# A two-layer decoder trunk on one core: the planner gets other lengths, and the side steps are spread between the parts of a pair

## The chip, the cores and the metric

The kernel runs on one core of one Trainium2 chip. The time is device microseconds (us) of one execution of the whole program; several runs are given by their median. TensorE is called PE, VectorE DVE, ScalarE ACT, GpSimd POOL and SyncE SP; SP issues nearly all DMAs. Smaller is better.

## The reference

The input is one sequence of 1024 tokens with 1024 features in float32. Two layers follow each other; each has a token mixer and a SwiGLU, and each of these four sub-layers reads a normed x that is scaled and shifted by vectors computed from a conditioning vector c (`mod`), and is added back with a gate from the same.

```python
for i in range(DEPTH):                      # 2
    mod = silu(c) @ ada_w[i] + ada_b[i]     # six vectors of 1024
    sh1, sc1, g1, sh2, sc2, g2 = split(mod, 6)
    h = rmsnorm(x, norm1_g[i]) * (1 + sc1) + sh1
    y = dsa_mixer(h) if i == 0 else short_conv_mixer(h)
    x = x + g1 * y
    h = rmsnorm(x, norm2_g[i]) * (1 + sc2) + sh2
    x = x + g2 * ((silu(h @ w_gate[i]) * (h @ w_up[i])) @ w_down[i])   # 2816 hidden
```

The first mixer is a sparse attention: eight index heads score every key for every query (`relu(qi . ki)`, weighted and summed), the 256 best keys of a query are kept, and 16 heads with 4 key heads attend to those only. The second mixer is a gated causal convolution of width 3: `(b * conv(c * u)) @ w_out`.

## The kernel before

**Planner.** The code doesn't call the engines. It records operations into a `Plan`, with the operations that each depends on, and a list scheduler (`drain`) then issues them: it keeps a modelled clock for PE, DVE, ACT, POOL and SP, takes at each step the engine that can start first, and on it the ready operation with the lowest priority number. The priority is the place in the program, or a number that the code sets (`plan.pri`). So the order of instructions on each engine follows from the lengths that `cost` and `record` give to operations, from the delays between engines (`LATENCY`, `SLACK`), from the landing time of a DMA (1.6 us beyond its transfer at 380 KB per us), and from `CHANGE`, a charge on PE when the form of the stationary operand changes. `copy` operations may go to ACT or DVE, as the modelled clock has it. On the chip, each engine runs its instructions in the order in which they were issued, and waits at each until its operands are there.

**Products.** Most products are float32 split into a rounded high part and a rest: `whi` (a cast, mostly ACT) and `wlo` (a subtraction, DVE), and three matmuls for each (`mm3`), 512 columns wide.

**Stages.** First x is read and turned, the first conditioning vectors are made, and h is formed. Then come the projections: the index keys, the index queries (`rope_pair`, stored to DRAM by `to_dram` as `qid` and loaded back by `index` as `q` in the tile `karena`), keys, queries and values. `index` computes the row products of index queries and keys (`pair_products`, two matmuls with 64 rows each side by side into the bank `ps_L`), ACT applies the relu, and DVE sums into `sc`. `select` finds the 256th best score by 31 rounds of counting, on DVE or ACT. Attention (`attend`) goes by blocks of 128 queries: row products into `ps_L`, mask and maximum on DVE (tiles `p`, `mx`), exponential on ACT, transposes on PE, copies `pf`, products with the values into `ps_o`. The out projection is laid between the later blocks.

**Tail.** The SwiGLUs and the convolution use products by halves with seven instead of eight block products (class `Pair`: `first`, `second`, `rest`, `third`, `fourth`; pairs that had two products made early finish in `done`). In the SwiGLU one gate pair and one up pair make a step of 256 hidden columns, eleven steps in all. `row_sums` and `hidden` store results (`t`, `hid`) to DRAM for the down product. Beside this run *side steps*: `side_step` loads a block `adaw` of the conditioning weights (SP, three buffers) and adds its product with c to an accumulator `cv` (DVE); after eight of them PE turns the accumulator (`ada_turned`, four transposes with `ident`, a reduction on DVE). The first SwiGLU makes six of the vectors (96 loads), the second one (16). From the ninth pair on, eight side steps (four in the second SwiGLU) are recorded after a pair's use.

Of the kernel before, what the change touches and what calls it, by code (L numbers as in the profile page):

```python
# [161 lines left out]
class Plan:  # L162
# [4 lines left out]
    WINDOW = 3.41  # L167
    BIAS = 0.8
    CHANGE = 0.15
    STAY = 4.0  # L170

    def __init__(self, nc, tc):
        self.nc, self.tc, self.pri, self.count = nc, tc, None, 0
        for e in self.ENGINES:
            setattr(self, e, Engine(self, e))
        self.free = dict.fromkeys(self.ENGINES, 0.0)
        self.soon = {e: [] for e in self.ENGINES}
        self.now = {e: [] for e in self.ENGINES}
        self.dma = self.window = self.busy = 0.0
        self.slow = 2.0  # L180
        self.gate = self.form = None
# [25 lines left out]
    def cost(self, eng, fn, out, ins, kw):  # L207

        n = out.free
        if fn == "dma_start":  # L210
            if eng == "gpsimd":
                return 0.85, 1.6
            inside = len(ins) == 1 and all(r.store.alloc is not None for r in ins + [out])
            return {"sync": 0.65 if inside else 0.475, "scalar": 0.1}[eng], 1.6
        if eng == "tensor":
            if fn == "transpose":
                return 0.107, 0.0
            if ins[1].dtype in (F32R, BF16):
                return max(n, 64) * 17 / 38400.0, 0.0
            return max(n * 4, 512) / (4800.0 if HD in (ins[0].free, ins[0].shape[0]) else  # L220
                                      2400.0), 0.0
# [3 lines left out]
        if eng == "scalar":  # L225
            return 0.03 + 0.95e-3 * n + (0.09 if "accum_out" in kw else 0.0) + 0.1 * aps, 0.0
# [30 lines left out]
    def matmuls(self, calls, rate, start=True, stop=True):  # L257
# [9 lines left out]
        op = Op("tensor", rate * calls[0][0].free, emit, (self.pri, self.count))  # L267
# [5 lines left out]
    def record(self, eng, fn, args, kw, other=None):  # L273
# [17 lines left out]
        if fn == "dma_start":  # L291
            op.lat = lat + shaped.free * shaped.shape[0] * 4 / 380e3
# [99 lines left out]
    def drain(self, *pools):  # L392

        held = []
        while any(p.pending for p in pools) if pools else True:
# [44 lines left out]
            if op.lat:  # L440
                self.dma = max(self.dma, end) + (op.lat - 1.6)
                end = self.dma + 1.6
                if e == "sync":
                    self.free[e] = max(self.free[e], self.dma - 2.5)
# [11 lines left out]
HW = 512  # L456
# [354 lines left out]
class Attention:  # L811
# [225 lines left out]
    def to_dram(self, t, dram, j, two, half, sl):  # L1037
        rows = dram.part_of((half, j, two))[2 * P * j:2 * P * (j + 1), sl]
        self.nc.sync.dma_start(rows.rearrange("(h a q) t -> a h q t", a=2, q=32)[two], t)
# [90 lines left out]
    def pair_products(self, q, k, wd, use):  # L1130

        for c0 in range(0, wd, HW):
# [4 lines left out]
            self.plan.matmuls([(ps[r], q[rows[r]], k[rows[r], cs]) for r in range(2)], 2.057e-3)  # L1137
# [227 lines left out]
class Tail:  # L1365
# [4 lines left out]
    EARLY, KEPT, SIDE = 10, 4, (8, 4)  # L1370
# [4 lines left out]
    def __init__(self, tk, ada_w, xspill):  # L1375
        self.tk, self.nc, self.plan, self.ada_w = tk, tk.nc, tk.plan, ada_w
        plan = tk.plan
        plan.pri = None
# [137 lines left out]
    def side_steps(self, layer):  # L1516
        for _ in range(self.SIDE[layer]):
            self.side_step()
# [175 lines left out]
    def pairs(self, pairs, use):  # L1694

        last = None
        for n, p in enumerate(pairs):
            if p.began:
                use(n, p.done())
                continue  # L1700
            p.first()
            if last is not None:
                last.fourth()
            p.second()
            if last is not None:
                use(n - 1, last.third())
            p.rest()
            last = p
# [3 lines left out]
    def ffn(self, layer, w_gate, w_up):  # L1712
# [4 lines left out]
        def use(n, rows):  # L1717
# [17 lines left out]
            if n >= 8:  # L1735
                self.side_steps(layer)
# [11 lines left out]
    def conv(self, w_in):  # L1748
# [14 lines left out]
        def conved(n, cs, us):  # L1763
            for f in range(2):
                i = 2 * n + f
                cw = [tk.vec[:, R_CW + j * 8 + i:R_CW + j * 8 + i + 1] for j in range(3)]
                for half in range(NH):
# [8 lines left out]
                    nc.vector.tensor_scalar(y, z[:, 0:HW], cw[0], None, op0=ALU.mult)  # L1776
# [20 lines left out]
    def run(self, w_gate, w_up, w_down, w_in, w_out, out):  # L1797
        self.side = self.side_list([(0, 5), *((1, j) for j in range(5))])
        self.ffn(0, w_gate[0], w_up[0])
# [3 lines left out]
        self.side = self.side_list([(1, 5)])  # L1803
        self.ffn(1, w_gate[1], w_up[1])
# [157 lines left out]
```

## Time and profile before

| | |
|---|---|
| median of 3 runs | 2303.0 us (2300.35 to 2303.5) |
| the profiled execution | 2300.25 us, span 2298.5 us |
| busy share of the span: PE, DVE, ACT | 97%, 79%, 49% |
| mean granted clock of PE | 0.991 |
| moved by DMA | 356.39 MB, mean 155 GB/s |

A row of a stretch of time gives its length and, for each engine, how long it was busy and with how many instructions, then the clock that PE was granted (1.00 is full speed), the busy share of the 16 DMA engines, and GB/s. A row of the timeline gives the start, the length, the engine, the operation with its output and inputs, and in brackets how long the engine stood idle before and what ended that. A row of waits gives who waited for whom, the sum, how many times, and the longest. A row of a group gives the busy time and mean length of its instructions, and the idle time just before them. Matmuls overlap in PE, so their lengths (0.39 us) are longer than the distance of their starts.

### The profile page before, as it was taken

How to read it: one execution, taken by the hardware profiler on the slowest of the kernel's cores; microseconds unless marked ns; L12 is line 12 of the kernel's file. 1: busy time of each engine (PE TensorE's matmuls, PEld its weight loads, DVE VectorE, ACT ScalarE, POOL GpSimd, SP SyncE). 2: the span in 40 equal slices, each digit the busy share in tenths (PEclk: the TensorE clock that was granted, in tenths of full speed). 3: DMA queues.
4: the chain of work that ended last, by engine and by line, in shares of the span. 5: the costliest groups of instructions: out<-in, count | busy, mean ns of one | idle time of the engine just before them, and what ended most of it. 6: DMA issues, size and time to landing. Idle time of an engine off the chain costs nothing.

```text
span 2298.5 us, 33032 instructions
## 1 busy us (share of the span) xinstructions
PE 2239.1 (97%) x11686; PEld 1812.2 (79%) x11686; DVE 1822.3 (79%) x3716; ACT 1116.4 (49%) x2137; POOL 5.6 (0%) x19
## 2 busy tenths in 40 slices
PE   7999999999999999999999999999999999999998
PEld 6667876876798887778888887778888878888887
DVE  6879999776478898888678899886798976667774
ACT  4576899756755333333344552234453233343444
POOL 0000000000000000000000000000000000000000
PEclk8999999999999999999999999999999999999999
DMA  8423343332244566655984154325345633349733
GB/s 299 128 65 94 91 120 98 105 92 66 74 126 136 175 209 201 221 185 187 362 298 168 55 147 129 115 89 173 110 140 181 197 107 110 111 152 388 275 125 97
DMA packets 334192, 356.39 MB, mean 155 GB/s; under 512 B 18089, under 2 KB 218826, under 8 KB 334026
## 3 DMA queue, kind: packets, MB, share of 16 engines
q1 hardware_dynamic: 332586, 352.96, 47.6%
q8 instruction: 92, 1.51, 0.3%
q10 hardware_dynamic: 1440, 1.31, 0.2%
q14 instruction: 74, 0.61, 0.1%
HBM read 282.64 MB, written 71.57 MB: 154 GB/s over the span
## 4 chain that ended last, share of the span: by engine, by line
PE 62%; DVE 18%; DMA 9%; issue 8%; ACT 2%; SPq 0%; POOL 0%; DVEq 0%; ACTq 0%; POOLq 0%
PE ps_x L244 24%; PE ps_mm L244 17%; PE ps_z L244 12%; PE ps_sm L244 5%; DVE s L244 3%; DVE u L244 3%; DVE wlo L244 3%; DMA raw<-in_ffn_w_gate_dram 2%; PE ps_L L244 2%; PE ps_o L244 2%; DVE v L244 2%; DMA adaw<-in_ada_w_dram 2%; DMA raw<-in_conv_w_in_dram 2%; DMA raw<-in_ffn_w_up_dram 2%; DVE cv L244 2%
## 5 line engine op out<-in xcount | busy, mean ns | idle before, releaser
L244 ACT CAST whi<-s 128x512 fp32r<-128x512 f32 x312 | 193.1, 621 | 452.5 <-issue 128.0
L244 PE MATMUL ps_x<-t,whi 128*128 128x512 f32 x1016 | 315.2, 391 | 8.6 <-ACT v L244 7.3
L244 ACT CAST whi<-raw 128x512 fp32r<-128x512 f32 (+1 forms) x245 | 149.6, 617 | 273.6 <-PE ps_z L244 68.7
L244 DVE TENSOR_TENSOR wlo<-s,whi 128x512 fp32r<-128x512 f32 x312 | 212.8, 685 | 46.5 <-ACT whi L244 45.9
L244 PEld LDWEIGHTS ps_x<-t,whi 128*128 128x128 f32 x1016 | 189.2, 188 | 50.6 <-ACT v L244 9.4
L244 DVE TENSOR_TENSOR wlo<-raw,whi 128x512 fp32r<-128x512 f32 (+1 forms) x254 | 172.7, 683 | 66.1 <-ACT whi L244 65.3
L244 PE MATMUL ps_x<-t,wlo 128*128 128x512 f32 x508 | 198.2, 390 | 0.2 <-DVE wlo L244 0.2
L244 PE MATMUL ps_x<-h,whi 128*128 128x512 f32 x536 | 165.6, 390 | 0.0
L244 PE MATMUL ps_z<-t,whi 128*128 128x512 f32 x488 | 150.3, 389 | 0.0
L244 DVE CUSTOM_DVE_ANT_0 p<-ps_L,bias 128x512 f32<-128x512 f32 (+3 forms) x192 | 99.7, 551 | 38.4 <-PE ps_L L244 23.7
L244 PE MATMUL ps_z<-h,whi 128*128 128x512 f32 x408 | 125.8, 389 | 1.1 <-DVE u L244 1.1
L244 PE MATMUL ps_mm<-h,whi 128*128 128x512 f32 x400 | 123.8, 390 | 1.4 <-DVE v L244 1.4
L244 ACT ACTIVATE p<-p,nm,qsc 128x128 f32<-128x128 f32 (+7 forms) x128 | 111.6, 874 | 24.6 <-DVE nm L244 21.5
L244 PE MATMUL ps_x<-ph,whi 128*128 128x512 f32 x396 | 122.1, 389 | 0.0
L244 DVE TENSOR_TENSOR s<-raw 128x512 f32<-128x512 f32 x112 | 76.6, 686 | 52.6 <-DMA raw<-in_ffn_w_gate_dram 27.0
L244 PEld LDWEIGHTS ps_x<-h,whi 128*128 128x128 f32 x536 | 100.4, 188 | 20.7
L244 ACT ACTIVATE junk<-sc,bs 128x896 bf16<-128x896 f32 (+3 forms) x124 | 109.7, 885 | 14.0 <-DVE bs L244 9.5
L244 PEld LDWEIGHTS ps_x<-t,wlo 128*128 128x128 f32 x508 | 95.3, 188 | 21.2 <-DVE wlo L244 1.0
L244 PEld LDWEIGHTS ps_z<-t,whi 128*128 128x128 f32 x488 | 91.6, 188 | 19.0
L244 PE MATMUL ps_x<-h,wlo 128*128 128x512 f32 x268 | 104.6, 390 | 1.7 <-DVE wlo L244 1.7
L244 DVE TENSOR_TENSOR u<-u 128x512 f32<-128x512 f32 x152 | 102.9, 684 | 2.4 <-ACT u L244 0.8
L244 PE MATMUL ps_mm<-hhi,whi 128*128 128x512 f32 (+2 forms) x240 | 93.5, 391 | 1.6 <-ACT hhi L244 1.6
(379 smaller groups left out, 5403.4 us busy)
## 6 DMA issues: line engine op xcount, KB each, us to landing
adaw<-in_ada_w_dram SPq DMA_DIRECT2D x160, 256.0 KB
ph<-in_ffn_w_down_dram SPq DMA_DIRECT2D x66, 512.0 KB
raw<-in_ffn_w_gate_dram SPq DMA_DIRECT2D x54, 512.0 KB
raw<-in_ffn_w_up_dram SPq DMA_DIRECT2D x54, 512.0 KB
rt<-t SPq DMA_DIRECT2D x80, 256.0 KB
raw<-in_conv_w_in_dram SPq DMA_DIRECT2D x34, 512.0 KB
hid<-u SPq DMA_DIRECT2D x52, 256.0 KB
rt<-hid SPq DMA_DIRECT2D x48, 256.0 KB
```

Of the source, the lines that this page charges most:

```text
L244: f(*[a.get() if isinstance(a, Ref) else a for a in args], **{k: a.get() if isinstance(a, Ref) else a for k, a in kw.items()})
```

## The change

Numbers of the planner are changed, most of them lengths: a DMA lands 2.2 us after its transfer, not 1.6; a change of form costs 0.097 us, not 0.15; copies and other work on ACT are shorter, transposes a little longer, narrow float32 matmuls shorter; a row product has a fixed part and a part by its width; in the tail a transfer goes at 300 KB per us, not 380. The store of a projection (`to_dram`) counts as landed 4 us later still. Two things are moved by hand: side steps are recorded between the parts of a pair, two at each place in the first SwiGLU and one in the second, and the convolution's product with its first tap is done by ACT instead of DVE.

```diff
+    LANDING = 2.2
-    CHANGE = 0.15
+    CHANGE = 0.097
...
-            if ins[1].dtype in (F32R, BF16):
-                return max(n, 64) * 17 / 38400.0, 0.0
-            return max(n * 4, 512) / (4800.0 if HD in (ins[0].free, ins[0].shape[0]) else
-                                      2400.0), 0.0
+            if ins[1].dtype in (F32R, BF16):
+                return 0.0133 + n / 2400.0, 0.0
+            return 0.112 if n < 64 else n * 4 / 2400.0, 0.0
...
-            return 0.03 + 0.95e-3 * n + (0.09 if "accum_out" in kw else 0.0) + 0.1 * aps, 0.0
+            if "accum_out" in kw:
+                return 0.17 + 0.845e-3 * n + 0.1 * aps, 0.0
+            return 0.04 + 0.83e-3 * n + (0.04 if out.dtype == F32R else 0.0), 0.0
...
-            op.lat = lat + shaped.free * shaped.shape[0] * 4 / 380e3
+            op.lat = lat + shaped.free * shaped.shape[0] * 4 / self.rate
...
-                self.dma = max(self.dma, end) + (op.lat - 1.6)
-                end = self.dma + 1.6
+                self.dma = max(self.dma, end) + (op.lat - self.LANDING)
+                end = self.dma + self.LANDING + op.late
...
-        self.nc.sync.dma_start(rows.rearrange("(h a q) t -> a h q t", a=2, q=32)[two], t)
+        self.nc.sync.dma_start(rows.rearrange("(h a q) t -> a h q t", a=2, q=32)[two], t).late = 4.0
...
-            self.plan.matmuls([(ps[r], q[rows[r]], k[rows[r], cs]) for r in range(2)], 2.057e-3)
+            self.plan.matmuls([(ps[r], q[rows[r]], k[rows[r], cs]) for r in range(2)], 1.648e-3, base=0.104)
...
-        plan.pri = None
+        plan.pri, plan.rate = None, 300e3
...
         for n, p in enumerate(pairs):
+            side = self.side_steps if n >= 8 else lambda: None
             if p.began:
-                use(n, p.done())
+                side()
+                rows = p.done()
+                side()
+                use(n, rows)
+                side()
                 continue
             p.first()
+            side()
             if last is not None:
                 last.fourth()
             p.second()
+            side()
             if last is not None:
                 use(n - 1, last.third())
+            side()
             p.rest()
+            side()
             last = p
...
-            if n >= 8:
-                self.side_steps(layer)
...
-                    nc.vector.tensor_scalar(y, z[:, 0:HW], cw[0], None, op0=ALU.mult)
+                    nc.scalar.activation(y, z[:, 0:HW], AF.Copy, scale=cw[0])
```

Three places show how this moves instructions. The first is PE at the second batch of index row products (`ps_L<-karena`, the rows 128x512 and 128x128 are one pair of heads of the fifth query block; `hhi`, `hlo` with `whi`, `wlo` is the projection of the keys, `blk` with `qsq` their squared norms). Before:

```order
L244 MATMUL ps_mm<-hhi_257,whi 128x512
L244 MATMUL ps_mm<-hlo_638,whi 128x512
L244 MATMUL ps_L<-karena 128x512 x2
L244 MATMUL ps_L<-karena 128x128 x2
L244 MATMUL ps_mm<-hhi_257,wlo 128x512
L244 MATMUL ps_sm<-blk_87,qsq 128x4
L244 MATMUL ps_mm<-hhi_258,whi 128x512
```

And now:

```order
L246 MATMUL ps_sm<-blk_87,qsq 128x4 x7
L246 MATMUL ps_mm<-hhi_258,wlo 128x512
L246 MATMUL ps_mm<-hhi_258,whi 128x512
L246 MATMUL ps_mm<-hlo_504,whi 128x512
L246 MATMUL ps_mm<-hhi_258,wlo 128x512
L246 MATMUL ps_mm<-hhi_258,whi 128x512
L246 MATMUL ps_mm<-hlo_504,whi 128x512
L246 MATMUL ps_L<-karena 128x512 x2
L246 MATMUL ps_L<-karena 128x128 x2
```

The row products moved from before the last matmul of the first half of the keys (`hhi_257`) into the second half (`hhi_258`), past 21 wide and 8 small matmuls.

The second is DVE at the same place, where `sc<-s,wiT` is the first sum over index heads, `bs` are the steps of `select`, and `ssk`, `rst`, `rk`, `rb` are the norm of the keys. Before:

```order
L244 TENSOR_TENSOR bs<-bs 128x2
L244 SCALAR_TENSOR_TENSOR bs<-bs 128x2
L244 TENSOR_SCALAR bs<-bs 128x2
L244 TENSOR_SCALAR sc_240<-s_1179,wiT 128x640
L244 SCALAR_TENSOR_TENSOR sc_240<-s_1186,wiT,sc_240 128x640
L244 TENSOR_TENSOR sw<-rt,S 128x512
L244 TENSOR_TENSOR rt<-rt,sw 128x512
```

And now:

```order
L246 COPY ssk<-ps_sm 128x16
L246 TENSOR_SCALAR bs<-bs 128x2
L246 TENSOR_SCALAR rst<-ssk 128x16
L246 RECIPROCAL rst<-rst 128x16
L246 TENSOR_TENSOR bs<-bs 128x2
L246 TENSOR_TENSOR rst<-rst 128x16
L246 SCALAR_TENSOR_TENSOR bs<-bs 128x2
L246 TENSOR_TENSOR rst<-rst 128x16
L246 TENSOR_SCALAR bs<-bs 128x2
L246 TENSOR_SCALAR rst<-rst 128x16
L246 TENSOR_TENSOR rk<-rst 128x16
L246 COPY rb<-rk 128x512
```

The row `TENSOR_SCALAR sc_240` follows behind these now; the norm of the keys, which stood behind it, has moved ahead of it.

The third is SP in the sixth step of the first SwiGLU (`raw` are weights of the gate and up products, 512 KB each, `adaw` side steps, 256 KB each). Before:

```order
L244 DMA raw<-in_ffn_w_gate_dram 128x8x128
L244 DMA adaw<-in_ada_w_dram 128x512 x7
L244 DMA raw<-in_ffn_w_gate_dram 128x8x128
L244 DMA adaw<-in_ada_w_dram 128x512 x4
L244 DMA hid_11_129<-u 128x512
L244 DMA raw<-in_ffn_w_up_dram 128x8x128
L244 DMA adaw<-in_ada_w_dram 128x512
L244 DMA hid_11_107<-u 128x512
L244 DMA adaw<-in_ada_w_dram 128x512 x4
```

And now:

```order
L246 DMA raw<-in_ffn_w_gate_dram 128x8x128
L246 DMA adaw<-in_ada_w_dram 128x512 x4
L246 DMA raw<-in_ffn_w_gate_dram 128x8x128
L246 DMA adaw<-in_ada_w_dram 128x512 x3
L246 DMA hid_11_129<-u 128x512
L246 DMA raw<-in_ffn_w_up_dram 128x8x128
L246 DMA hid_11_107<-u 128x512
L246 DMA adaw<-in_ada_w_dram 128x512 x3
```

Between the two gate loads four side loads stand instead of seven, in the next steps five instead of seven or eight.

More of the change, by code (lines that the diff above doesn't have):

```diff
@@ L179, in __init__ @@
         self.dma = self.window = self.busy = 0.0
-        self.slow = 2.0
+        self.slow, self.rate = 2.0, 380e3
         self.gate = self.form = None
@@ L211, in cost @@
             if eng == "gpsimd":
-                return 0.85, 1.6
+                return 0.85, self.LANDING
             inside = len(ins) == 1 and all(r.store.alloc is not None for r in ins + [out])
-            return {"sync": 0.65 if inside else 0.475, "scalar": 0.1}[eng], 1.6
+            return {"sync": 0.65 if inside else 0.475, "scalar": 0.1}[eng], self.LANDING
         if eng == "tensor":
             if fn == "transpose":
-                return 0.107, 0.0
+                return 0.11, 0.0
             if ins[1].dtype in (F32R, BF16):
-                return max(n, 64) * 17 / 38400.0, 0.0
-            return max(n * 4, 512) / (4800.0 if HD in (ins[0].free, ins[0].shape[0]) else
-                                      2400.0), 0.0
+                return 0.0133 + n / 2400.0, 0.0
+            return 0.112 if n < 64 else n * 4 / 2400.0, 0.0
         psum = any(r.store.space == PSUM for r in ins + [out])
@@ L255, in tt, with matmuls @@
         return self.record("vector", "tensor_tensor", (out, a, b), {"op": op})
-    def matmuls(self, calls, rate, start=True, stop=True):
+    def matmuls(self, calls, rate, start=True, stop=True, base=0.0):
         kw = {"start": start, "stop": stop}
@@ L266, in matmuls @@
         self.count += 1
-        op = Op("tensor", rate * calls[0][0].free, emit, (self.pri, self.count))
+        op = Op("tensor", base + rate * calls[0][0].free, emit, (self.pri, self.count))
         op.form = tuple(calls[0][1].shape)
@@ L1365 @@
 class Tail:
-    EARLY, KEPT, SIDE = 10, 4, (8, 4)
+    EARLY, KEPT = 10, 4
     FIRST, SECOND = ("h11", "h21"), ("h22", "t1", "t2", "t3", "t4")
@@ L1514, in side_step, with side_steps @@
         tk.ada_step(w, k, self.acc[-1])
-    def side_steps(self, layer):
-        for _ in range(self.SIDE[layer]):
+    def side_steps(self):
+        for _ in range(self.rate):
             self.side_step()
@@ L1798, in run @@
         self.side = self.side_list([(0, 5), *((1, j) for j in range(5))])
+        self.rate = 2
         self.ffn(0, w_gate[0], w_up[0])
@@ L1803, in run @@
         self.side = self.side_list([(1, 5)])
+        self.rate = 1
         self.ffn(1, w_gate[1], w_up[1])
```

## The prediction

> **What bounds the kernel now.** I read the page's engine totals first, then the busy time of each engine by stage, then the waits of TensorE (PE) in each stage, and last the single gaps in order of time. The page:
>
> ```profile
> span 2298.5 us, 33032 instructions
> PE 2239.1 (97%) x11686; PEld 1812.2 (79%) x11686; DVE 1822.3 (79%) x3716; ACT 1116.4 (49%) x2137; POOL 5.6 (0%) x19
> PE 62%; DVE 18%; DMA 9%; issue 8%; ACT 2%; SPq 0%; POOL 0%; DVEq 0%; ACTq 0%; POOLq 0%
> ```
>
> PE is busy for 2239.1 of 2298.5 us and carries 62% of the chain that ended last. The change takes no matmul away, so it can win only the 59.4 us in which PE stands still, what the throttled clock costs behind such a standstill, and what the order of small matmuls costs. Where these 59.4 us lie is told by nine stretches: start, projections and index, attention, first FFN (its down part from 1110), convolution, its output, second FFN, end. The columns are the stretch, its length, and busy time (with instructions) of PE, of PE's weight loads, DVE, ACT and POOL, then granted clock, DMA share and GB/s.
>
> ```profile
> 0.00:110.00 110.00, 91.98 (x474) 72.29 (x475) 82.57 (x189) 52.23 (x93) 2.24 (x14) 0.89 0.67 222
> 110.00:290.00 180.00, 173.45 (x853) 131.96 (x852) 161.21 (x469) 138.91 (x304) 3.33 (x5) 0.97 0.30 83
> 290.00:670.00 380.00, 368.45 (x3219) 286.17 (x3218) 290.71 (x940) 284.20 (x631) 0.00 (x0) 1.00 0.30 93
> 670.00:1110.00 440.00, 429.65 (x1921) 353.30 (x1920) 375.42 (x623) 163.18 (x284) 0.00 (x0) 1.00 0.60 192
> 1110.00:1310.00 200.00, 199.97 (x891) 165.75 (x891) 157.16 (x256) 91.50 (x159) 0.00 (x0) 1.00 0.63 226
> 1310.00:1560.00 250.00, 245.73 (x1079) 200.07 (x1078) 224.90 (x389) 89.41 (x156) 0.00 (x0) 1.00 0.41 120
> 1560.00:1750.00 190.00, 189.66 (x850) 156.54 (x849) 150.17 (x250) 91.21 (x155) 0.00 (x0) 1.00 0.46 141
> 1750.00:2070.00 320.00, 317.64 (x1404) 262.32 (x1403) 227.28 (x365) 112.16 (x194) 0.00 (x0) 1.00 0.43 140
> 2070.00:2299.00 229.00, 222.61 (x1011) 183.78 (x1009) 152.92 (x241) 93.60 (x166) 0.00 (x0) 1.00 0.63 220
> ```
>
> Length less PE's busy time gives the idle time: 18.0, 6.6, 11.6, 10.4, 0.0, 4.3, 0.3, 2.4 and 6.4 us. The start and the end (24.4 us together) wait for first loads and last stores, whose rows the new order hardly moves. So about 35 us are within reach, in five places, and I price each.
>
> **The change part by part.** The numbers of the planner (landing 2.2 for 1.6 us, form change 0.097 for 0.15, 300 for 380 KB/us in the tail, shorter row products, copies and exponentials, 4 us more behind a projection's store) issue nothing themselves. They only move instructions, and both programs have the same matmuls. So their cost is what they do to waits.
>
> *The second index batch* is where I see it best. Here the rows are PE's row product, DVE's first use of it, the DMAs ahead of both, and two stretches of 4 us, with one of 50 us behind them.
>
> ```profile
> 121.48 7.24 DMA qid<-rt
> 128.86 3.06 DMA karena<-qid
> 131.97 2.50 PE L244 MATMUL ps_L<-karena 64*128 64x512 f32 x8 [4.60 <-DMA karena<-qid]
> 135.38 0.55 DVE L244 TENSOR_SCALAR sc<-s,wiT 128x640 f32<-128x640 f32 x1 [6.29 <-ACT s L244]
> 132.00:136.00 4.00, 4.00 (x13) 2.57 (x14) 0.55 (x1) 1.91 (x6) 0.00 (x0) 0.50 0.43 120
> 150.00:200.00 50.00, 49.26 (x232) 30.37 (x229) 49.34 (x101) 33.96 (x72) 2.36 (x3) 1.00 0.13 34
> ```
>
> The store of the index queries and the load back take 7.24 and 3.06 us. PE stands 4.60 us at the first row product, and then runs 4 us at half clock, which loses 2.0 more; DVE stands 6.29 us. In the new order this row product stands behind 21 wide matmuls and 8 small ones more. The stretch from 1110 above has 891 matmuls, nearly all wide, in 199.97 us, 0.22 us each, so this is about 5 us of PE work, and DVE gets the norm of the keys (eight small steps and the spread of it) ahead of its index rows. The wait is covered if the store isn't later. What is late next is DVE: from 150 on it is busy 49.34 of 50 us, so what PE wins is kept only as far as DVE has filled its own hole. Against it, the first index batch moves 16 wide matmuls back, 3.6 us by the same 0.22. Bounds: 6.6 us won (gap and half clock), 3.6 us lost (first batch late, DVE the bound). I take 4 won, nearest to the gap's own row of 4.60, which has the work now put into it.
>
> *Attention (290 to 670).* PE's waits there are many and short; a row is engine and tile, what it waits for, sum, count, longest.
>
> ```profile
> PE ps_L L244 <- DVE mx L244: 4.9, 7, 1.9
> PEld ps_L L244 <- DVE mx L244: 10.3, 18, 2.3
> ```
>
> The planner priced a full row product at 1.053 us and 0.15 for the form, and has now 0.948 and 0.097. It thus places the product nearer to its true turn, but moves many DVE rows by a place or two, in both directions; stretches of equal kind on PE stay as many (364 runs before, 367 now, counted in the two programs). Bounds: all 11.6 us idle won; or the 10.3 us once more lost. No row says which, so I stay near the middle: 2 won.
>
> *First FFN: side steps.* Each side step is a load (adaw) on SP and one pass on DVE. 96 of them stood eight together behind a pair's use; now two stand between any two parts of a pair. Both programs have 96 passes; by first-FFN step (two pairs each) DVE has 2, 8, 8, 24, 21, 9, 16, 8 of them before and 4, 6, 7, 20, 18, 18, 17, 6 now. Side work by itself is not what makes PE wait: the first three rows here are all engines in three stretches of 40 us, the next three DVE's side steps alone in the same.
>
> ```profile
> 840.00:880.00 40.00, 37.33 (x166) 30.28 (x165) 39.97 (x68) 11.89 (x21) 0.00 (x0) 1.00 0.62 204
> 960.00:1000.00 40.00, 35.56 (x155) 28.26 (x155) 33.79 (x56) 11.74 (x21) 0.00 (x0) 1.00 0.57 186
> 1000.00:1040.00 40.00, 40.00 (x182) 33.07 (x181) 34.35 (x57) 13.97 (x24) 0.00 (x0) 1.00 0.60 199
> 840.00:880.00 40.00, 8.07 (x12) 1.00 0.62 204
> 960.00:1000.00 40.00, 9.32 (x13) 1.00 0.57 186
> 1000.00:1040.00 40.00, 11.44 (x16) 1.00 0.60 199
> ```
>
> With 16 steps PE lost nothing, with 13 it lost 4.4 us. What counts is what stands in front of a late item:
>
> ```profile
> 931.79 9.86 SPq L244 DMA_DIRECT2D adaw<-in_ada_w_dram  x8
> 941.92 0.38 SPq L244 DMA_DIRECT2D raw<-in_ffn_w_gate_dram  x1
> 947.36 0.69 DVE L244 TENSOR_TENSOR s<-raw 128x512 f32<-128x512 f32 x1 [2.06 <-DMA raw<-in_ffn_w_gate_dram]
> 981.86 0.63 ACT L244 ACTIVATE v<-v 128x512 f32<-128x512 f32 x1 [2.72 <-DVE v L244]
> 983.54 0.73 PE L244 MATMUL ps_x<-t,whi 128*128 128x512 f32 x2 [2.73 <-ACT v L244]
> PE ps_x L244 <- ACT v L244: 6.3, 4, 2.7
> ```
>
> Eight adaw issues in a row (each waits for one of three buffers, thus for DVE) hold SP 9.86 us; the weights behind them are issued at 941.92 and DVE waits until 947.36. And at 983.54 PE waits for ACT's copy out of its bank, ACT stands at a silu, and that waits for DVE, which has side steps ahead. Four such waits make 6.3 of the 10.4 us. In the new order 4 or 5 adaw stand between the two gate loads instead of 7 or 8, so the second is issued at least 3/8 of 9.86 us, 3.7 us, earlier than now, more than the 2.06 that DVE waited; and no step has 24. What speaks against: a pair with all its parts now takes ten steps instead of eight, and four first-FFN steps in a row hold 17 to 20. DVE did 68 instructions in 39.97 us, 0.59 each; the new steps have 66, 58, 60 and 55, thus 39, 34, 35 and 32 us, against 14 products of 12 matmuls, 38 us of PE. Only the first is over, by one. Bounds: 10.4 won; or 4.4 lost in each of four steps, 17.6 less the present 10.4, 7.2 lost. I take 4 won, some of the four waits for ACT and the ones behind late weights. The second FFN, with 2.4 us of the same kind (its steps go from 2, 6, 8 to 4, 7, 5), I take 1 won, between 2.4 won and 2.4 lost.
>
> *Convolution.* Sixteen products by the first tap go from DVE to ACT. The rows are one of their three groups, a like operation on ACT, and a stretch of this stage.
>
> ```profile
> L244 DVE TENSOR_SCALAR u<-u,vec 128x512 f32<-128x512 f32 x8 | 3.8, 476 | 0.0
> L244 ACT ACTIVATE u<-u,mod 128x512 f32<-128x512 f32 x8 | 5.7, 724 | 2.2 <-DVE u L244 2.2
> 1435.00:1485.00 50.00, 48.85 (x211) 38.97 (x211) 46.17 (x83) 13.88 (x24) 0.00 (x0) 1.00 0.36 107
> ```
>
> DVE gives up 16 times 0.476, 7.6 us at most, and ACT takes at most 16 times 0.724, 11.6 us. ACT is busy 13.88 of 50 us here, which hides it; if it were not, each tap would wait 0.7 us in DVE's row of taps, but no matmul needs these rows. DVE at 46.17 of 50 is what PE waits for, 4.3 us in the stage. Bounds: 4.3 won, 2 lost (half of the idle again, for the new hop DVE to ACT and back). I take 2 won.
>
> The sum: 4 + 2 + 4 + 1 + 2 = 13 us won. The profiled execution took 2300.25 us, 1.75 more than its span; less 13 it would be 2287.25. The median of the runs is 2303.0, 2.75 above the profiled one, so the median comes to **2290 us**.
>
> **Rivals.** *Slower, by attention.* If the shorter row product brings PE to it too early, more products find their bank still read by DVE. Attention has 96 of them (eight for each block of 128 queries, twice as many in the last four blocks), and by the row above 18 wait, 10.3 us, 0.57 each. If 48 waited, that would be 27.4 us, 17.1 more; with the other 11 us won it is 6 lost, 2309. It decides against the change from 45 of 96 on, (10.3 + 11 + 4.6) / 0.57. For it speaks that DVE's rows change places all through this stretch; against it, that the kinds on PE alternate as often as before and both prices moved by only 0.16 us a product. Chance 0.14.
>
> *No change.* PE's 4.6 us at the index turn into DVE's time behind it, where DVE is at 49.34 of 50, and the first FFN's waits move with ten side steps a pair instead of going: 0 to 4 won, about 2301. The three stretches above, where waits don't follow the number of steps, speak for it; the 9.86 us block on SP, which is gone, against. Chance 0.19.
>
> *A larger gain.* It comes if loads land as the plan now has them: 2.2 + 512 KB at 300 KB/us, 3.95 us. Then no DVE pass stands in front of late weights, and 6.6 + 5.8 (half of attention's idle) + 10.4 + 4.3 + 2.4 = 29.5 us go: 2273. The rows of the chain and of DVE's waits:
>
> ```profile
> 821.36 5.79 DMA raw<-in_ffn_w_gate_dram
> DVE s L244 <- DMA raw<-in_ffn_w_gate_dram: 27.0, 17, 3.7
> DVE s L244 <- DMA raw<-in_ffn_w_up_dram: 18.0, 12, 3.9
> ```
>
> A weight load took 5.79 us, 1.8 more than even the new plan has. So the plan is still short and some of the 29 waits stay. Chance 0.13. The Trainium skill (DMA: Bandwidth & Descriptors, "Anatomy of one DMA — SWDGE (gpsimd) path") fits one DMA at about 2.0 us and its bytes over 436 GB/s; an estimate by it gives 3.2 us for such a load, under the plan's price, and this larger gain would then be the likely one. The trace differs with its 5.79 us, on another queue and beside other transfers, and the measurement decides.
>
> **How the numbers follow.** Faster as summed 0.54, larger gain 0.13, no change 0.19, slower 0.14. About 0.2% (4.6 us) is what a measurement of this kernel can tell from no change, so faster is 0.54 + 0.13 = 0.67, same 0.19, slower 0.14. The likeliest case alone runs from 2281 to 2298. With both other cases the range is 2275 to 2306: the lower end takes nearly all of the larger gain, the upper end the no-change case and the first half of attention's loss. One in ten is left out on either side.
>
> **What would show it.** Right: no gap over 2 us at the first row product of the second index batch, and a clock of 1.00 behind it; in the first FFN an idle time of PE of 4 to 8 us and no wait of ACT for v over 2 us; DVE under 46 of 50 us in the convolution. Wrong: PE idle over 14 us from 290 to 670 with waits for mx at its head; the 10 us of the first FFN unchanged, with waits for adaw or weights on DVE; or DVE idle before 150 and full after it, with PE's gap gone and the stage no shorter.

## The result, and the profile after

The changed kernel takes 2281.98 us (median of 4 runs, 2281.04 to 2284.37), the kernel before beside it 2301.68. The ratio is 0.991, with a 95% interval of 0.989 to 0.993: 0.9% faster. The profiled execution of after took 2284.37 us with a span of 2282.7; that of before had a span of 2298.5. So the medians differ by 19.7 us and the two traces by 15.8; what has to be found are the 15.8, since only the traces show stages. The experiments below ran in three groups, each on a chip of its own, where the kernel before took 2307.5, 2307.4 and 2309.2 us; so their ratios are compared, not their times. The profiled execution of one experiment (e10) was disturbed, so that no time of its trace is used, only the order of its instructions.

The page of after, its lines as quoted of before:

```profile
span 2282.7 us, 33002 instructions
PE 2237.3 (98%) x11686; PEld 1820.7 (80%) x11686; DVE 1820.4 (80%) x3705; ACT 1131.4 (50%) x2148; POOL 4.1 (0%) x19
PE 92%; DVE 4%; ACT 2%; DMA 1%; issue 1%; SPq 0%; ACTq 0%; DVEq 0%
```

PE has the same 11686 matmuls and the same work (2237.3 against 2239.1 us), and now carries 92% of the chain that ended last instead of 62%. What went are DVE (18 to 4%), loads (9 to 1%) and issue (8 to 1%). The same nine stretches, their bounds moved with the stages:

```profile
0.00:110.00 110.00, 91.49 (x461) 76.04 (x463) 78.33 (x180) 48.54 (x86) 1.76 (x13) 0.80 0.68 221
110.00:290.00 180.00, 172.06 (x837) 128.78 (x833) 163.07 (x465) 137.88 (x298) 2.33 (x6) 0.97 0.31 81
290.00:670.00 380.00, 370.97 (x3234) 289.85 (x3234) 294.17 (x958) 287.20 (x641) 0.00 (x0) 0.99 0.30 93
670.00:1094.00 424.00, 424.00 (x1913) 351.66 (x1912) 372.41 (x616) 165.45 (x282) 0.00 (x0) 1.00 0.62 197
1094.00:1311.00 217.00, 216.97 (x965) 179.78 (x965) 171.53 (x278) 99.66 (x174) 0.00 (x0) 1.00 0.63 216
1311.00:1542.00 231.00, 227.06 (x1000) 187.04 (x999) 207.00 (x356) 92.36 (x156) 0.00 (x0) 0.99 0.42 125
1542.00:1740.00 198.00, 198.00 (x886) 163.54 (x885) 153.76 (x255) 93.31 (x159) 0.00 (x0) 1.00 0.46 144
1740.00:2055.00 315.00, 315.00 (x1395) 260.84 (x1394) 226.47 (x362) 114.23 (x194) 0.00 (x0) 1.00 0.44 142
2055.00:2283.00 228.00, 221.79 (x1008) 183.16 (x1006) 153.64 (x242) 92.75 (x163) 0.00 (x0) 1.00 0.65 220
```

Idle time of PE (length less busy) is now 18.5, 7.9, 9.0, 0.0, 0.0, 3.9, 0.0, 0.0 and 6.2 us. The first FFN's 10.4 us are gone altogether, the index stage has 7.9 (6.6 before).

Idle time alone misses what a throttled clock costs, and fixed bounds cut stages. So I read a stage's length from PE's own rows: the start of the first matmul of each stage in the timeline. (The planner lays work of neighbouring stages beside each other at the seams, so a stage's length here is the distance between two such starts and nothing more.) These are the rows of after:

```profile
59.99 0.70 PE L246 MATMUL ps_mm<-hhi,whi 128*72 128x512 f32 x1 [1.01 <-ACT hhi L246]
311.99 0.72 PE L246 MATMUL ps_L<-karena,qst 64*128 64x128 f32 x8
672.66 0.63 PE L246 MATMUL ps_x<-h,whi 128*128 128x512 f32 x2
1093.74 0.71 PE L246 MATMUL ps_x<-ph,whi 128*128 128x512 f32 x2
1310.79 0.61 PE L246 MATMUL ps_x<-h,whi 128*128 128x512 f32 x2
1542.09 0.85 PE L246 MATMUL ps_x<-u,cv 128*128 128x512 f32 x3
1640.67 0.95 PE L246 MATMUL ps_sm<-ones,u 128*128 128x1 f32 x8
```

In order: first projection (index keys), first attention product, first FFN, its down part, convolution, the convolution's output, the sum of squares for the second FFN's norm. The differences of neighbouring rows are the stages; the last runs to the end of the span. The same rows of before and of the experiments give this table (us):

| run | start | projections, index | attention | first FFN, gate and up | its down part | convolution | its output | second FFN to end |
|---|---|---|---|---|---|---|---|---|
| before | 56.3 | 252.2 | 362.6 | 433.9 | 217.1 | 232.4 | 99.0 | 645.1 |
| after | 60.0 | 252.0 | 360.7 | 421.1 | 217.1 | 231.3 | 98.6 | 642.0 |
| e1 spreading alone | 58.5 | 252.6 | 362.8 | 440.1 | 217.1 | 231.0 | 99.0 | 645.8 |
| e2 all but spreading | 59.7 | 251.7 | 360.8 | 422.3 | 217.1 | 231.4 | 98.8 | 642.1 |
| e3 no 4 us behind a store | 59.5 | 253.4 | 361.4 | 421.1 | 217.1 | 232.6 | 98.6 | 642.0 |
| e4 first tap on DVE | 60.2 | 252.1 | 360.7 | 421.1 | 217.1 | 234.7 | 98.6 | 642.0 |
| e5 old lengths of loads | 60.7 | 250.3 | 363.3 | 437.3 | 217.1 | 231.2 | 99.7 | 642.2 |
| e6 lengths of loads alone | 59.5 | 258.5 | 367.0 | 422.3 | 217.0 | 242.0 | 98.5 | 641.9 |
| e7 380 KB/us in the tail | 57.4 | 252.1 | 360.8 | 421.6 | 217.1 | 227.2 | 98.5 | 641.9 |
| e8 3 us behind a store | 59.3 | 248.2 | 358.7 | 421.1 | 217.1 | 231.3 | 98.6 | 642.1 |
| e9 e7 and e8 together | 58.6 | 248.5 | 359.4 | 426.0 | 217.1 | 227.6 | 98.5 | 642.6 |
| e11 2.0 us, 3.5 us, 380 | 57.9 | 247.8 | 365.5 | 427.2 | 217.1 | 226.3 | 98.4 | 642.0 |
| e12 e9, side steps in bursts | 60.0 | 249.5 | 359.4 | 421.0 | 217.1 | 227.2 | 98.6 | 642.2 |

Before to after: start 3.7 lost, projections and index 0.2 won, attention 1.9, first FFN 12.8, convolution 1.1, its output 0.4, second FFN 3.1; together 15.8. The start isn't counted as a loss: in after, e2, e4 and e7, whose stages up to the first attention product agree within 0.4 us, it varies from 57.4 to 60.2, and e1, with the program of before there, has 58.5.

*First FFN.* Before, ten loads of gate and up weights stand in the chain of work that ended last. These are the first three:

```profile
766.30 6.36 DMA raw<-in_ffn_w_gate_dram
775.94 6.36 DMA raw<-in_ffn_w_up_dram
791.47 5.25 DMA raw<-in_ffn_w_gate_dram
```

Of after there is none in it. DVE's waits for loaded weights between 670 and 1105 us, before (five rows of L244) and after (four of L246):

```profile
DVE s L244 <- DMA raw<-in_ffn_w_gate_dram: 15.4, 8, 3.7
DVE s L244 <- DMA raw<-in_ffn_w_up_dram: 10.6, 7, 3.9
DVE cv L244 <- DMA adaw<-in_ada_w_dram: 10.5, 16, 1.7
DVE whi L244 <- DMA raw<-in_ffn_w_gate_dram: 3.3, 2, 2.0
DVE whi L244 <- DMA raw<-in_ffn_w_up_dram: 2.4, 1, 2.4
```

```profile
DVE s L246 <- DMA raw<-in_ffn_w_gate_dram: 5.2, 5, 1.4
DVE whi L246 <- DMA raw<-in_ffn_w_gate_dram: 1.4, 1, 1.4
DVE cv L246 <- DMA adaw<-in_ada_w_dram: 0.7, 2, 0.4
DVE whi L246 <- DMA raw<-in_ffn_w_up_dram: 0.3, 1, 0.3
```

42.2 us of waiting became 7.6. SP's long blocks of side loads, which I had named as a cause, have not gone, though. This is one of after:

```profile
877.54 9.13 SPq L246 DMA_DIRECT2D adaw<-in_ada_w_dram  x5
```

Five side loads hold SP for 9.13 us, about as long as eight did before (9.86 us), and PE has no wait behind them. So the waits went while the blocks stayed. Whether the spreading or the lengths did it, the two traces alone don't tell.

*Index.* The second batch no longer waits; instead PE stands still 67 us later. The first fence is the batch's first product, the 4 us that ran at half clock before, and the 50 us behind; the second ACT's last cast of weights ahead of PE's wait, the subtraction on DVE for which PE waits, and PE; the third PE's two stretches of 10 us there.

```profile
137.34 1.35 PE L246 MATMUL ps_L<-karena 64*128 64x512 f32 x8
132.00:136.00 4.00, 4.00 (x26) 3.57 (x26) 3.41 (x8) 3.17 (x8) 0.00 (x0) 1.00 0.47 137
150.00:200.00 50.00, 50.00 (x239) 31.02 (x235) 48.50 (x99) 33.79 (x73) 1.17 (x4) 1.00 0.11 32
```

```profile
199.88 0.62 ACT L246 CAST whi<-raw 128x512 fp32r<-128x512 f32 x1 [1.56 <-PE ps_mm L246]
210.42 0.69 DVE L246 TENSOR_TENSOR wlo<-raw,whi 128x512 fp32r<-128x512 f32 x1
211.16 0.79 PE L246 MATMUL ps_mm<-hhi,wlo 128*128 128x512 f32 x1 [6.51 <-DVE wlo L246]
```

```profile
200.00:210.00 10.00, 3.23 (x21) 2.27 (x19) 8.46 (x30) 8.82 (x18) 0.00 (x0) 0.79 0.68 176
210.00:220.00 10.00, 8.84 (x29) 7.08 (x30) 9.33 (x35) 7.83 (x17) 0.00 (x0) 0.69 1.09 189
```

ACT's four casts there are done by 200.50 at the latest, but DVE comes to the first of the four subtractions only at 210.42, behind its steps of the search for the 256th score and of the turning of keys. PE waits 6.51 us and then starts at a granted clock of 0.69 (the next rows take 0.63 us instead of 0.39). Before, the stretch 200 to 210 has PE busy for all of its 10 us.

*Convolution.* DVE is relieved as forecast, 42.93 of 50 us instead of 46.17 (the stage lies 11 us earlier now; a stretch moved by as much has 43.01). But PE is busy for less of it too, 46.05 us instead of 48.85, for it has a new wait, again for a subtraction on DVE:

```profile
1435.00:1485.00 50.00, 46.05 (x195) 37.01 (x194) 42.93 (x75) 13.97 (x24) 0.00 (x0) 0.97 0.39 116
1453.73 0.50 PE L246 MATMUL ps_z<-t,wlo 128*128 128x512 f32 x1 [3.18 <-DVE wlo L246]
```

### The profile page after: what moved, and what is told of

It reads as the page before. It is cut to its first block, busy times and chain, and to the rows that moved or that the text cites. A ratio compares the mean times of both kernels' runs of the same rounds, so it can differ in the third digit from the quotient of the medians.

```text
span 2282.7 us, 33002 instructions
## 1 busy us (share of the span) xinstructions
PE 2237.3 (98%) x11686; PEld 1820.7 (80%) x11686; DVE 1820.4 (80%) x3705; ACT 1131.4 (50%) x2148; POOL 4.1 (0%) x19
## 4 chain that ended last, share of the span: by engine, by line
PE 92%; DVE 4%; ACT 2%; DMA 1%; issue 1%; SPq 0%; ACTq 0%; DVEq 0%
PE ps_x L246 33%; PE ps_mm L246 28%; PE ps_z L246 18%; PE ps_sm L246 6%; PE ps_L L246 4%; PE ps_o L246 3%; ACT junk L246 1%; DVE u L246 0%; DMA raw<-in_conv_w_in_dram 0%; DVE p L246 0%; DMA xs<-in_x_dram 0%; DVE wlo L246 0%; DVE s L246 0%; ACT p L246 0%; DVE sc L246 0%
## 5 line engine op out<-in xcount | busy, mean ns | idle before, releaser
L246 ACT CAST whi<-s 128x512 fp32r<-128x512 f32 x311 | 192.7, 621 | 388.5 <-DVE s L246 116.0
L246 PE MATMUL ps_x<-t,whi 128*128 128x512 f32 x1016 | 314.4, 390 | 0.0
L246 ACT CAST whi<-raw 128x512 fp32r<-128x512 f32 (+1 forms) x228 | 139.5, 618 | 252.4 <-PE ps_z L246 84.4
L246 DVE TENSOR_TENSOR wlo<-s,whi 128x512 fp32r<-128x512 f32 x312 | 213.3, 688 | 47.5 <-ACT whi L246 46.3
L246 DVE TENSOR_TENSOR wlo<-raw,whi 128x512 fp32r<-128x512 f32 (+1 forms) x254 | 173.2, 686 | 75.2 <-ACT whi L246 74.4
L246 PEld LDWEIGHTS ps_x<-t,whi 128*128 128x128 f32 x1016 | 190.8, 188 | 39.6
L246 PE MATMUL ps_x<-t,wlo 128*128 128x512 f32 x508 | 198.1, 390 | 0.0
L246 PE MATMUL ps_x<-h,whi 128*128 128x512 f32 x536 | 165.6, 390 | 0.0
L246 PE MATMUL ps_z<-t,whi 128*128 128x512 f32 x488 | 150.9, 390 | 0.0
L246 DVE CUSTOM_DVE_ANT_0 p<-ps_L,bias 128x512 f32<-128x512 f32 (+3 forms) x192 | 100.3, 553 | 39.8 <-PE ps_L L246 16.7
L246 PE MATMUL ps_z<-h,whi 128*128 128x512 f32 x408 | 126.0, 390 | 0.0
L246 PE MATMUL ps_mm<-h,whi 128*128 128x512 f32 x400 | 123.3, 389 | 0.0
L246 PE MATMUL ps_x<-ph,whi 128*128 128x512 f32 x396 | 122.0, 389 | 0.0
L246 ACT ACTIVATE p<-p,nm,qsc 128x128 f32<-128x128 f32 (+7 forms) x128 | 111.4, 873 | 21.2 <-DVE nm L246 20.0
L246 ACT ACTIVATE junk<-sc,bs 128x896 bf16<-128x896 f32 (+3 forms) x124 | 109.4, 883 | 17.4 <-DVE bs L246 12.5
L246 PEld LDWEIGHTS ps_x<-h,whi 128*128 128x128 f32 x536 | 100.2, 188 | 20.5
L246 PEld LDWEIGHTS ps_x<-t,wlo 128*128 128x128 f32 x508 | 95.5, 188 | 20.2 <-DVE wlo L246 0.2
L246 PEld LDWEIGHTS ps_z<-t,whi 128*128 128x128 f32 x488 | 91.8, 188 | 19.4 <-ACT whi L246 0.3
L246 DVE TENSOR_TENSOR u<-u 128x512 f32<-128x512 f32 x152 | 103.5, 687 | 2.6 <-ACT u L246 0.8
L246 PE MATMUL ps_x<-h,wlo 128*128 128x512 f32 x268 | 104.6, 390 | 0.0
L246 PE MATMUL ps_mm<-hhi,wlo 128*128 128x512 f32 (+2 forms) x240 | 93.0, 389 | 7.3 <-DVE wlo L246 7.2
L246 PE MATMUL ps_z<-t,wlo 128*128 128x512 f32 x244 | 95.6, 392 | 3.9 <-DVE wlo L246 3.9
```

Of the source, the lines that this page charges most:

```text
L246: f(*[a.get() if isinstance(a, Ref) else a for a in args], **{k: a.get() if isinstance(a, Ref) else a for k, a in kw.items()})
```

## The experiments

Theory after the first comparison: the spreading of the side steps won the first FFN. Rival: the planner's lengths did.

**e1: the kernel before, with the spreading alone.**

```diff
+            side = self.side_steps if n >= 8 else lambda: None
...
             p.first()
+            side()
             if last is not None:
                 last.fourth()
             p.second()
+            side()
...
-            if n >= 8:
-                self.side_steps(layer)
```

> The kernel before, with only the side steps spread between the parts of a pair; all the planner's lengths, the store's added time and the convolution's first tap stay as before. Theory (the spreading won the first FFN): the gate and up part of the first FFN takes about 421 us instead of 433.9, the second FFN 2 to 3 us less, and the total is 2285 to 2289 us, 13 to 16 under the 2301.7 of before. Rival (the planner's lengths, above all the longer loads, won it): the first FFN's part stays at 430 to 434 us and the total within 3 us of 2301.7. The start, the index part and attention are as before by both.

Measured: ratio 1.0011 (1.0001 to 1.0022), no gain. The first FFN takes 440.1 us, 6.2 more than before, the second 645.8. PE is busy 421.63 of the 435 us from 670 on, where after has all 435:

```profile
670.00:1105.00 435.00, 421.63 (x1880) 346.55 (x1880) 370.06 (x612) 158.12 (x276) 0.00 (x0) 0.99 0.59 185
```

The theory falls: with the old lengths, spreading costs. Nor did it shorten SP's blocks; the longest in this run has eight side loads and takes 10.95 us.

**e2: the changed kernel, with the side steps in bursts as before.** The edit is e1's, backwards.

> The changed kernel, with the side steps put back as before (eight in a row behind a pair's use in the first FFN, four in the second). Theory (the spreading won the first FFN): its gate and up part is back at 430 to 436 us with PE's waits for ACT's v, total 2294 to 2299 us. Rival (the planner's lengths won it): that part stays within 3 us of 421, total 2282 to 2286. If each alone gives most of it, both e1 and this one lie under 2290.

Measured: ratio 0.9897 (0.988 to 0.9913), as good as the changed kernel. The first FFN takes 422.3 us. Blocks on SP are there as in after:

```profile
926.01 8.56 SPq L246 DMA_DIRECT2D adaw<-in_ada_w_dram  x6
```

The stage is 1.2 us longer than in after. So the rival holds: the lengths won the first FFN. What SP's blocks cost is not shown apart, since none of these four programs is without them; but PE's waits are all but gone here too (0.7 us) with the blocks in place.

**e3: the changed kernel without the 4 us behind a store.**

```diff
-        self.nc.sync.dma_start(rows.rearrange("(h a q) t -> a h q t", a=2, q=32)[two], t).late = 4.0
+        self.nc.sync.dma_start(rows.rearrange("(h a q) t -> a h q t", a=2, q=32)[two], t)
```

> The changed kernel, without the 4 us that the planner adds behind a store of projected rows. Theory (that number moves a wait and takes none away): PE waits some 4 to 5 us at the first row product of the second index batch again, the 6.5 us wait for wlo near 204 us is gone, and the total is within 3 us of the changed kernel's 2282. Rival 1 (the number wins the 4.6 us and the stall at 204 comes from other lengths): total 2287 to 2291, both waits there. Rival 2 (the stall with its half clock costs more than the wait it replaced): total 2274 to 2278.

Measured: ratio 0.9915 (0.9898 to 0.9931). PE's waits between 60 and 310 us, the longest two:

```profile
PE ps_mm L246 <- ACT qsq L246: 3.5, 1, 3.5
PE ps_L L246 <- DMA karena<-qid: 2.9, 1, 2.9
```

The wait for the load back is there again (2.9, not the 4 to 5 expected), the one for `wlo` at 204 is gone, a wait of 3.5 for ACT has come, and index with attention takes 614.7 us against 612.7. That is the theory: the number moved a wait and took hardly anything away.

**e4: the changed kernel with the first tap on DVE.**

```diff
-                    nc.scalar.activation(y, z[:, 0:HW], AF.Copy, scale=cw[0])
+                    nc.vector.tensor_scalar(y, z[:, 0:HW], cw[0], None, op0=ALU.mult)
```

> The changed kernel, with the convolution's first tap back on DVE. Theory (16 taps of 0.476 us off DVE are worth 1 to 2 us in the convolution): the stage of 231.3 us takes 232 to 233.5, total 2283 to 2285. Rival (DVE isn't what PE waits for there, and the new 3.2 us wait for wlo at 1450 to 1500 us comes with the tap on ACT): the stage takes 228 to 230, total 2278 to 2281. The rest of the program is unchanged up to 1310 us by both.

Measured: the convolution takes 234.7 us, 3.4 more than with the tap on ACT; the other stages are unchanged. In the whole time (0.9904, 0.9887 to 0.9921) this can't be told. In this program the tap is thus worth more than the expected 1 to 2 us. How much of the 3.4 is DVE's relief and how much the changed order isn't shown apart. The 3.18 us wait isn't in this run; waits of PE for ACT's casts of weights stand in its place, up to 2.0 us each:

```profile
PE ps_z L246 <- ACT whi L246: 2.3, 2, 2.0
PE ps_mm L246 <- ACT whi L246: 1.3, 1, 1.3
```

New theory, from e1 and e2 and DVE's waits: the two lengths of loads (landing 2.2 us, 300 KB/us) won the first FFN.

**e5: the changed kernel with both lengths of loads as before.**

```diff
-    LANDING = 2.2
+    LANDING = 1.6
...
-        plan.pri, plan.rate = None, 300e3
+        plan.pri = None
```

> The changed kernel, with the planner's two numbers for loads back as before (landing 1.6 us, 380 KB/us to the end); side steps spread, all else as changed. New theory (with the longer loads the planner puts DVE's work on fresh weights later in its row, so DVE no longer stands before a load): the first FFN's gate and up part goes back to 430 to 441 us (421 changed; 440 in the first run, which had old lengths and spread side steps), DVE again waits 15 us or more there for loaded weights, the second FFN takes 644 us or more instead of 642, ratio to the kernel before 0.997 to 1.001. Rival (the lengths of ACT's copies and of form changes did it): the part stays at 421 to 424, ratio 0.988 to 0.993.

Measured: ratio 0.9985 (0.9972 to 0.9998), the first FFN takes 437.3 us, and DVE stands before the loads again:

```profile
DVE s L246 <- DMA raw<-in_ffn_w_gate_dram: 16.6, 10, 4.2
DVE s L246 <- DMA raw<-in_ffn_w_up_dram: 15.7, 8, 3.8
```

The second FFN stays at 642.2 against what I expected (644 or more): there the other parts of the change are enough.

**e6: the kernel before, with only the two lengths of loads changed.** The edit is e5's, backwards, with the two attributes that hold the numbers.

> The kernel before, with only the planner's two numbers for loads changed (landing 2.2 us, 300 KB/us in the tail). New theory (these two are what won the first FFN): gate and up part 421 to 425 us, ratio 0.991 to 0.996, the rest from what the head does. Rival (loads are needed but not enough, the lengths of copies have to fit as well): that part 427 us or more, ratio 0.996 to 1.000.

Measured: the first FFN takes 422.3 us, 11.6 less than before, and the second 641.9, with all other numbers as before. The theory holds for these stages. But the ratio, expected at 0.991 to 0.996, is 0.9995 (0.9983 to 1.0007): index loses 6.3 us, attention 4.4, the convolution 9.6. In the convolution PE waits for DVE's split of the weights:

```profile
1324.00:1566.00 242.00, 231.07 (x1002) 186.31 (x1001) 214.55 (x374) 79.32 (x138) 0.00 (x0) 0.99 0.40 118
PE ps_x L245 <- DVE wlo L245: 3.1, 4, 1.5
PE ps_x L245 <- DVE whi L245: 2.9, 2, 1.5
PE ps_z L245 <- DVE wlo L245: 2.0, 2, 1.5
```

So the other parts of the change (lengths of copies and products, the 4 us, the tap) are worth some 20 us, not because they gain on before, but because they take back what the lengths of loads lose elsewhere.

**e7: the changed kernel with 380 KB/us in the tail.** The edit is the second half of e5's.

> The changed kernel, with 380 KB/us in the tail as before and the landing of 2.2 us kept; the program up to the tail is the same. A load of 512 KB is then 3.6 us long in the plan, against 3.95 changed, 2.98 before and 5 to 6 in the trace. If the gain grows with the length in the plan: first FFN's part 424 to 430 us. If the landing alone is enough: 420 to 423, ratio as the changed kernel's, 0.990. If the rate is what counts: 430 or more, ratio 0.995 or more.

Measured: ratio 0.9875 (0.9854 to 0.9897). The first FFN takes 421.6 us, so beside the other new lengths the landing is enough there, and the convolution only 227.2: PE is busy 48.98 of 50 us where after has 46.05.

```profile
1435.00:1485.00 50.00, 48.98 (x213) 39.15 (x212) 44.77 (x79) 15.18 (x26) 0.00 (x0) 1.00 0.36 104
```

The 300 KB/us thus won nothing in the first FFN and cost 4.1 us in the convolution.

**e8: the changed kernel with 3 us behind a store.** The edit is the number alone.

> The changed kernel, with 3 us instead of 4 behind a store of projected rows. Theory (the 6.5 us wait for wlo near 204 us comes from the row order that these 4 us set, and another number gives another order): that wait is under 3 us, PE still doesn't wait for the load at the second index batch by more than 2 us, and the total is 4 to 8 us under the changed kernel, ratio 0.986 to 0.989. Rival (the 6.5 us are DVE's work, which has to be done somewhere before the index is finished): the wait comes back in other places, attention begins within 2 us of where it did, ratio 0.990 to 0.992.

Measured: ratio 0.9868 (0.9841 to 0.9896). The stall at 204 us is gone, and the second batch has no wait over 2 us either:

```profile
200.00:210.00 10.00, 9.39 (x48) 7.22 (x46) 8.75 (x29) 6.91 (x13) 0.00 (x0) 1.00 0.61 162
```

Index takes 248.2 us and attention 358.7, together 5.8 less than after. The rival, that DVE's work must be done somewhere anyway, fails: with another order it fits beside PE.

**e9: e7 and e8 together**, both edits in one.

> The changed kernel, with 3 us behind a store and 380 KB/us to the end. By the separate runs each of the two wins in a place of its own: the head as with 3 us alone (attention's first product 248 us behind the projections' first matmul, the tail 359 us later), the first FFN's gate and up part 421 to 422, the convolution 227 instead of 231. If they add up: ratio 0.983 to 0.986, 3 to 5 us under either alone. Rival (the plan's rows change places again when both are set): one of the two gains is gone, ratio 0.986 to 0.989.

Measured: ratio 0.987 (0.9852 to 0.9889): the rival. Index, attention and convolution are as in the two runs, but the first FFN takes 426.0 us, 4.4 more than in e7, though both plan with the same numbers from the tail on; only what stands ahead of it differs. PE's one wait over 0.2 us there:

```profile
PE ps_x L246 <- DVE v L246: 3.2, 1, 3.2
```

**e10: the kernel before, with landing 2.2 us from the tail on.** The edit is one number, `plan.pri, plan.LANDING = None, 2.2`, where the tail begins.

> The kernel before, with one number changed: from the tail on the planner takes 2.2 us for a load's landing (1.6 until then, so the program up to the tail is the same as before's). Theory: that number alone wins the first FFN, its gate and up part takes 421 to 423 us instead of 433.9, the second FFN 642 instead of 645; the convolution loses 0 to 10 us, since it lost 9.6 with both numbers for loads and the old lengths of copies. Ratio 0.992 to 0.998. Rival (300 KB/us or the other lengths are needed too): the first FFN's part stays above 427 us, ratio 0.997 to 1.002.

Measured: ratio 1.0006 (0.9995 to 1.0018). That is outside what I expected of the theory and inside what I expected of the rival. But the run can't decide between them, because the edit does more than I had said. The kernel records all operations first and issues them afterwards. The number is set before the tail is recorded, but nothing has been issued by then, so it holds for the whole issuing, the start included. There it meets loads that were recorded with 1.6 us, and the planner then takes 0.6 us too little for the transfer of each. The order of the trace shows it. Before goes from the turning of x (`ps_mm<-ident,xs`) to `ps_L<-ident,nr` at 21.15 us; e10 makes four more matmuls of that turning and then the ten products `ps_sm<-ones,sc`. So it isn't known whether the landing alone, with the old lengths of copies, wins the first FFN.

**e11: the changed kernel with 2.0 us, 3.5 us and 380 KB/us**, three numbers.

> The changed kernel, with 2.0 us for a load's landing, 3.5 us behind a store and 380 KB/us to the end; all three near the values of the run before the last. If the numbers matter by how true they are, it is within 2 us of the run with 3 us and 380 KB/us (ratio 0.983 to 0.986). If they matter by which order they happen to give, the index part or attention differs by 3 us or more in either direction (0.981 to 0.990); the first FFN's part stays 421 to 424 by both, since 2.0 is still above the 1.6 that left DVE waiting.

Measured: ratio 0.989 (0.9872 to 0.9907). Attention takes 365.5 us, 6.1 more than e9, and the first FFN 427.2, where I had expected 421 to 424 by either reading. So numbers close to each other give orders that differ by 6 us in one stage.

**e12: e9, with the side steps in bursts as before**, by e2's edit.

> As the run with 3 us and 380 KB/us, with the side steps put back eight (second FFN four) in a row behind a pair's use. If the spreading wins something once the lengths are right: first FFN's part 1 to 2 us longer (422.5 to 424), ratio 0.0005 to 0.001 higher. If it is worth nothing: both parts within 0.7 us.

Measured: ratio 0.9859 (0.9841 to 0.9877), the lowest of all, and its interval doesn't touch the changed kernel's. I expected the first FFN to be 1 to 2 us longer than e9's or the same; it is 421.0 us, 5.0 shorter.

All runs but e10 together show what the length of a load does in the first FFN. The price is what the planner takes for 512 KB, landing and transfer; the waits are summed from 670 to 1105 us (DVE) and from 672 to 1090 us (PE).

| price, us | runs | DVE's waits for loads, us | PE's waits, us | first FFN, gate and up, us |
|---|---|---|---|---|
| 2.98 | before, e1, e5 | 42.2 to 44.7 | 9.3 to 13.4 | 433.9 to 440.1 |
| 3.38 | e11 | 29.4 | 4.3 | 427.2 |
| 3.58 | e7, e9, e12 | 19.1 to 24.1 | 0 to 3.2 | 421.0 to 426.0 |
| 3.95 | after, e2, e3, e4, e6, e8 | 7.6 to 13.8 | 0 to 0.7 | 421.1 to 422.3 |

DVE's waits fall with the price throughout, with the side steps spread (e1, e5, e7) or in bursts (before, e12, e2), and with the old lengths of copies (e6). PE's waits are all but gone while DVE still waits some 20 us, in e7 and e12. How a load's reader moved in DVE's row wasn't laid out for this stage; that it moved is taken from the planner's rule and these waits.

## Why the prediction was right, and where it was not

The time (2290 forecast, 2282 measured) lies in the range, and in the likeliest case's own range near its lower end. The signs of all terms held or came out near zero. That the sum came out is in part luck: the 4 us of the index didn't come, and the first FFN brought 8.8 more than its term, by another mechanism than the one priced. Step by step, from the traces of before and after:

- *Second index batch, 4 forecast, 0.2 measured.* The mechanism came as described: no gap at 137 and full clock behind it. What failed is the size of the gain. The prediction named DVE as late next, "busy 49.34 of 50 us", and still kept 4 of the 6.6 us. DVE's full row put one subtraction late, and PE's 6.51 us with the slow clock behind took the gain back. PE's gap gone and the stage no shorter is also half of a sign that was named for being wrong. e8 shows 4.0 us for this stage with the same idea and another number.
- *Attention, 2 forecast, 1.9 measured.* PE's weight loads wait for `mx` 9.7 us, 14 times (10.3, 18 times before). The term was set near the middle of its bounds, with no row for it, so that its number fits is luck. That this could as well have gone the other way is shown by e6 (4.4 lost) and e11 (2.9 lost): the slower rival's direction was real, its 17 us were not seen.

```profile
PEld ps_L L246 <- DVE mx L246: 9.7, 14, 1.8
```

- *First FFN, side steps, 4 forecast, 12.8 measured.* This is the step that failed in its mechanism. Spreading alone costs 6.2 us (e1), and beside the new lengths it won 1.2 (after against e2) or lost 5.0 (e9 against e12). SP's block, which the prediction calls gone, is there with PE's waits (9.86 us before, 10.95 in e1) and without them (9.13 in after). The count of side steps was wrong as well: a pair with all its parts has four places with two steps, thus eight as before, not ten. What won is in the prediction too, but as the larger-gain rival with a chance of 0.13: "Then no DVE pass stands in front of late weights". I had set it aside because a load takes 5.79 us, "1.8 more than even the new plan has". The runs show that the plan needn't reach the true length. With 2.98 us for 512 KB (1.6 us and 380 KB/us) DVE waits over 42 us and PE over 9; with 3.58 PE has 3.2 us of waits or less, though the chain's loads took 3.90 us and more. What is left of DVE's waiting is then covered by products that PE already has. The prediction's two rows of DVE's waits (27.0 and 18.0 us) are those of the whole program; 15.4 and 10.6 of them lie in the first FFN. The Trainium skill (DMA: Bandwidth & Descriptors, "Anatomy of one DMA — SWDGE (gpsimd) path") gives an estimate of 3.2 us for such a load, on the gpsimd path. The ten in the chain of before, on SP's queue, took 3.90 to 6.36, so the measurement stands; the old plan, with 2.98 us, was under either.
- Of the signs I had named for it, an idle time of PE of 4 to 8 us came out at 0.0. "No wait of ACT for v over 2 us" was a poor one: ACT still waits up to 3.4 us, and PE has no wait behind it.

```profile
ACT v L246 <- DVE v L246: 13.9, 11, 3.4
```

- *Second FFN, 1 forecast, 3.1 measured.* Under-sized; it comes with the lengths of loads alone (e6, 641.9) as with the others alone (e5, 642.2), and not with the spreading (e1, 645.8).
- *Convolution, 2 forecast, 1.1 measured.* I had one term of at least two. The tap is worth 3.4 us (e4); the 300 KB/us take 4.1 back (e7), by a wait that the prediction didn't price. The two together would lose 0.7, so other parts of the change won some 1.8; which ones no run shows.
- *Start, 0 forecast.* 3.7 us longer in the two traces, but it moves by 2.8 us from run to run with an equal program; no cause is shown.

## What to carry to other kernels

Where a planner with prices orders the work, judge a change of prices stage by stage, by the first matmul of each stage: here two numbers won 11.6 us in one stage, lost 9.6 in the convolution behind it and 10.7 in two others, and the whole time showed nothing (e6). A load priced too short puts its reader in front of other work on an in-order engine, and beside the other new lengths a price nearer the measured time by 0.6 us was enough (e7). Before a table is kept, try its neighbours: 3 for 4 us at one store and 380 for 300 KB/us, with the side steps left as they were, gave 1.4% under the kernel before instead of 0.9 (e12), though two good changes do not always add (e9), and two orders from nearly equal numbers can differ by 5 or 6 us in a stage (e9 and e12, e9 and e11).

## What I had not expected of the hardware

The start, up to the first projection, took from 57.4 to 60.2 us with programs whose next two stages agree to 0.4 us, and the kernel before took 2301.7 us beside the changed kernel and 2307 to 2309 in the three groups of experiments. No run shows the cause of either. Both are as large as half of the effects looked for here, which is why stages were compared and not sums.
